# Two additions of the down-weight sums: from VectorE to GpSimd

## The chip, the cores and the metric

The kernel runs on one core of a Trainium2 chip. The metric is the device time of one execution in microseconds (us). The kernel before took 927.64 us, the median of three runs (927.62 to 928.56).

A core has four computing engines, each with its own queue of instructions in program order: TensorE (PE; PEld is its loading of weights), VectorE (DVE), ScalarE (ACT) and GpSimd (POOL). Instructions on different engines wait for each other through semaphores. DMA transfers are issued from the queues of SyncE (SP), ScalarE and GpSimd. TensorE writes to the banks of PSUM; the other engines read these banks or work on SBUF.

## The reference

Two decoder layers on an input of 512 x 1024. Layer 0 mixes by multi-scale causal pooling, layer 1 by differential attention. After each mixer comes a dense FFN, and after each of these four parts a LayerNorm of the scaled residual:

```python
def _swiglu(x, w_gate, w_up, w_down):
    return (jax.nn.silu(x @ w_gate) * (x @ w_up)) @ w_down

for i in range(DEPTH):
    h = _multiscale_pool(...) if i % 2 == 0 else _diff_attention(...)
    x = _layernorm(ALPHA * x + h, ln_mix_g[i], ln_mix_b[i])
    x = _layernorm(ALPHA * x + _swiglu(x, w_gate[i], w_up[i], w_down[i]), ln_ffn_g[i], ln_ffn_b[i])
```

The width of the FFN is 2816, all in float32. The change concerns the FFN, in both layers.

## The kernel before

**Products.** A float32 product is made of three matmuls of a reduced 32-bit type. Each operand is split into a high part (a cast, ScalarE) and a low part (the difference to the operand, VectorE): high x high, high x low, low x high, added up in a PSUM bank. So every 128x1024 piece of a weight costs a cast on ScalarE (L716 for gate and up) and a subtraction on VectorE (L719), ahead of its matmuls.

**Gate and up.** The hidden rows, 22 blocks of 128, are taken in units: plain ones, and nine double ones in which the 2x2 blocks of a product are made by seven products in place of eight (Strassen's way; `strassen`, L995). The seven are P1, Q5, P6, Q3, P7, P2 and Q4; the first two of the nine units have P1 and P2 made ahead and run five. The products of a unit are collected in three PSUM banks: A takes P1, P6, P7 and Q4 one after the other, C takes Q5 and Q3, B takes P2. Between them, other engines copy or combine what a bank holds so far: ScalarE copies A after P1 (L1015), C after Q5 (L1017) and A after P6 (L1019); VectorE reads C after Q3 (L1024) and A after P7 (L1026). TensorE may go on writing to a bank only when that reading is done. The matmuls of one of these products (`half_product`, L919) are 24 of 128x256. Sums of weight pieces for the products are made on VectorE (L713). All this is ordered by hand: what the other engines do is written between the products, with the preparation of weights some products ahead (`ahead`, `do_step`).

**The sums for the down product.** The product with w_down that follows is made by seven products as well. It needs sums of the four quarters of w_down, by rows of two blocks: W00+W01, W01+W11, W00+W01+W11 and W00+W01+W10+W11. They are made while gate and up run, and kept in DRAM (`tsum`) until they are read back. This goes in eleven steps for each FFN, k = 0 to 10:

- `load_terms(k)` (L812), from GpSimd's queue: two DMAs (L823) bring the quarters of step k into a tile of 128 x 2 x 2 x 512, then a third (L824) adds two quarters onto the first half while it loads. The tile is a part of the hidden buffer that is not yet in use for even k below 10 (`hid` in the trace), else a tile of its own (`b`).
- `sum_terms(k)` (L827): two additions of 128x512 (L829, L830), which make the last two sums out of the second half of the tile and what the third DMA left; the second reads what the first wrote.
- At the next `catch_up`, one product later: two DMAs to `tsum` from ScalarE's queue (L834). The first stores the first half of the tile, which the additions only read, and the second the half that they wrote. Then `load_terms(k + 2)` is issued.

The steps stand at the units and products in SUMMED (L53): behind the units f1, f2, f3, p3 and p4, and within p5 to p10 behind one of their products. Two tiles are under way at a time: loading of step k+1 is issued before the additions of step k stand in program order, loading of step k+2 after them.

GpSimd has little else to do in the FFN: its queue holds the loads and, at the end of each stage, a power of 128x1 for LayerNorm (L235). It takes a part in splitting elsewhere (L160 with `low=nc.gpsimd`).

Of the kernel before, what the change touches and what calls it, by code (L numbers as in the profile page):

```python
# [16 lines left out]
ALU = mybir.AluOpType  # L17
# [61 lines left out]
def trunk(ctx, tc, x, wall, pscale, lam_p, subln, table, lng, lnb, band, first, onehot, out):  # L79
    nc = tc.nc  # L80
# [489 lines left out]
    def ffn(layer, late):  # L570
# [6 lines left out]
        tt = nc.vector.tensor_tensor  # L577
        with tc.tile_pool(name=f"ffn{layer}", bufs=1) as fp:
# [230 lines left out]
            def term_slice(k):  # L809
                return slice(k % 2 * 512, (k % 2 + 1) * 512)  # L810

            def load_terms(k):  # L812
                if k < HALF - 1:
                    c = down + 4 * (k // 2)
                    src = wall[c : c + 4][:, :, term_slice(k)].rearrange("(j r) p t -> p j r t", j=2)
                else:
                    src = wall[down + 20 : down + 22].rearrange("j p (r t) -> p j r t", r=2)
                if k % 2 == 0 and k < HALF - 1:
                    t = rows_of[:, :, 9:11, :]
                else:  # L820
                    t = fp.tile([P, 2, 2, 512], F32, tag="b", name=f"b{layer}_{k}")
                for j in range(2):
                    nc.gpsimd.dma_start(out=t[:, j], in_=src[:, j])  # L823
                nc.gpsimd.dma_start(out=t[:, 0], in_=src[:, :, 1], accum_op=ALU.add)  # L824
                terms[k] = t

            def sum_terms(k):  # L827
                t = terms.pop(k)
                tt(t[:, 1, 1], t[:, 0, 0], t[:, 1, 1], op=ALU.add)  # L829
                tt(t[:, 1, 0], t[:, 1, 1], t[:, 1, 0], op=ALU.add)  # L830
                yield
                dst = tsum[:, k // 2, :, term_slice(k)].rearrange("(j r) p t -> p j r t", j=2)
                for j in range(2):
                    nc.scalar.dma_start(out=dst[:, j], in_=t[:, j])  # L834
                if k + 2 < HALF - 1:
                    load_terms(k + 2)
                if k == HALF - 2:
                    load_terms(HALF - 1)
# [4 lines left out]
            def weight_sums():  # L843
                g = sum_terms(summed_rows[0])
                summed_rows[0] += 1
                next(g)
                behind.append(g)
# [841 lines left out]
```

## Time and profile before

| | before |
|---|---|
| median of the runs | 927.64 us |
| range of the runs | 927.62 to 928.56 us |
| the profiled execution, its own time | 928.3 us |
| its span, first to last instruction | 926.5 us |
| mean granted TensorE clock | 0.998 |

The profile is of one execution. "Busy" is the time in which an engine had an instruction running. A row of a group gives line, engine, operation, tiles written and read, the shape and the count, then the busy time in us and the mean of one in ns, then the idle time of the engine just before it and what ended it. A row of the timeline gives start, duration, engine, line, operation, tiles and shapes, and in brackets the idle time before and who ended it. A row of the waits gives who waited for whom, and us in total, times, and the longest. A q behind an engine's name is its queue, which issues DMAs and waits. In tile names, numbers of buffers are left out, and g_28h and g_28l are the high and low part of weight piece 28 of an FFN.

### The profile page before, as it was taken

What the parts mean: (1) busy time and instruction counts of PE and PEld (TensorE: products, weight loads), DVE (VectorE), ACT (ScalarE), POOL (GpSimd) and SP (SyncE); (2) the same over time, 40 slices, a digit from 0 to 9 for tenths busy, and PEclk for the clock granted to TensorE, in tenths of its full rate; (3) what the DMA queues carried; (4) which work ended last, traced back from release to release, by engine and by line L of the source; (5) the groups of instructions that cost most, each with busy time, mean ns of one, the idle gap of its engine ahead of it and who ended that gap; (6) DMA issues with size and microseconds to landing.
All of it is one profiled execution on the core that took longest, in us unless ns stands there. A gap on an engine that the chain in (4) does not pass through costs nothing. (4 is left out here: it accounts for less than half of the span.)

```text
span 926.5 us, 15034 instructions
## 1 busy us (share of the span) xinstructions
PE 916.4 (99%) x5806; PEld 826.6 (89%) x5806; DVE 804.0 (87%) x1163; ACT 529.2 (57%) x841; POOL 110.3 (12%) x129
## 2 busy tenths in 40 slices
PE   9999999999999999999999999999999999999996
PEld 8999999999988888888888888989999999988885
DVE  7998798998899998868889786877798998899988
ACT  6773354444555657667878854843454444565551
POOL 4121121110100001101111100201111110100001
PEclk9999999999999999999999999999999999999999
DMA  8388988787766587975665622568878877756553
GB/s 235 119 285 235 296 254 248 256 249 241 219 215 192 188 251 226 227 206 151 163 144 120 155 90 69 162 225 257 264 195 289 279 251 236 220 195 206 193 203 103
DMA packets 72518, 192.50 MB, mean 208 GB/s; under 512 B 14548, under 2 KB 14804, under 8 KB 72446
## 3 DMA queue, kind: packets, MB, share of 16 engines
q1 hardware_dynamic: 44572, 121.36, 39.7%
q0 software_dynamic: 15712, 46.93, 22.5%
q10 hardware_dynamic: 12162, 23.25, 6.8%
q8 instruction: 45, 0.74, 0.3%
q14 instruction: 27, 0.22, 0.1%
HBM read 166.33 MB, written 25.19 MB: 207 GB/s over the span
## 5 line engine op out<-in xcount | busy, mean ns | idle before, releaser
L713 DVE TENSOR_TENSOR raw<-raw,raw 128x1024 f32<-128x1024 f32 x52 | 63.3, 1221 | 0.7
L160 DVE TENSOR_TENSOR xs<-hid,xs 128x512 fp32r<-128x512 f32 x84 | 53.7, 641 | 0.0
L159 ACT CAST xs<-hid 128x512 fp32r<-128x512 f32 x84 | 48.5, 580 | 0.4 <-DVE hid L1044 0.4
L1322 ACT ACTIVATE p<-p,mn 128x128 f32<-128x128 f32 (+3 forms) x64 | 35.2, 552 | 14.1 <-DVE mn L1317 14.1
L823 POOL DMA_DIRECT2D b<-in_wall x24 | 17.9, 793 | 144.1 <-DMA tsum<-b 33.9
L1317 DVE CUSTOM_DVE_ANT_0 p<-s,bias 128x128 f32<-128x128 f32 (+3 forms) x64 | 28.0, 485 | 1.1 <-PE s L1302 1.1
L823 POOL DMA_DIRECT2D hid<-in_wall x20 | 15.0, 751 | 111.7 <-DMA tsum<-hid 47.4
L1024 DVE TENSOR_TENSOR hid<-C,hid 128x512 f32<-128x512 f32 x18 | 12.4, 690 | 16.0 <-PE C L919 12.7
L235 POOL TENSOR_TENSOR rs<-rs,mhalf 128x1 f32<-128x1 f32 x16 | 12.5, 783 | 104.1 <-DVE rs L234 97.1
L1019 ACT COPY hid<-A 128x512 f32<-128x512 f32 x18 | 10.6, 586 | 24.9 <-PE A L919 24.9
L286 ACT ACTIVATE y<-pt,bT,gT 128x128 f32<-128x128 f32 x40 | 15.0, 456 | 15.9 <-PE pt L272 15.8
L1017 ACT COPY hid<-C 128x512 f32<-128x512 f32 x18 | 10.6, 588 | 22.2 <-PE C L919 17.2
L226 DVE BATCH_NORM_STATS2 st<-res 128x6 f32<-128x512 f32 x32 | 22.2, 695 | 1.1
L824 POOL DMA_DIRECT2D b<-in_wall x12 | 14.8, 1230 | 59.6 <-DMA b<-in_wall 59.6
L1026 DVE TENSOR_TENSOR hid<-hid,A 128x512 f32<-128x512 f32 x18 | 12.3, 682 | 10.6 <-PE A L919 10.6
L1031 ACT ACTIVATE sg<-A 128x512 f32<-128x512 f32 x18 | 10.7, 595 | 18.7 <-PE A L919 18.7
L1336 DVE SCALAR_TENSOR_TENSOR p<-p,sm,p 128x128 f32<-128x128 f32 (+3 forms) x32 | 17.6, 552 | 1.1
L713 DVE TENSOR_TENSOR more<-more,raw 128x1024 f32<-128x1024 f32 x15 | 18.3, 1220 | 0.2
L777 ACT CAST xs<-hid 128x1024 fp32r<-128x1024 f32 x8 | 8.4, 1052 | 14.3 <-DVE hid L786 8.7
L265 DVE TENSOR_TENSOR res<-res,gb 128x512 f32<-128x512 f32 (+1 forms) x20 | 16.0, 799 | 0.7
L160 POOL TENSOR_TENSOR sql<-sq,sqh 128x512 fp32r<-128x512 f32 x7 | 9.3, 1325 | 60.5 <-ACT sqh L159 60.5
L264 DVE TENSOR_TENSOR res<-res,gb 128x512 f32<-128x512 f32 (+1 forms) x20 | 15.8, 791 | 0.0
(1237 smaller groups left out, 3582.4 us busy)
## 6 DMA issues: line engine op xcount, KB each, us to landing
raw<-in_wall SPq DMA_DIRECT2D x120, 512.0 KB, 5.7
r<-tsum SPq DMA_DIRECT2D x40, 512.0 KB, 3.9
b<-in_wall POOLq DMA_DIRECT2D x36, 512.0 KB, 6.1
hid<-in_wall POOLq DMA_DIRECT2D x30, 512.0 KB, 5.8
r<-in_wall SPq DMA_DIRECT2D x30, 512.0 KB, 4.3
tsum<-b ACTq DMA_DIRECT2D x24, 512.0 KB, 4.4
tsum<-hid ACTq DMA_DIRECT2D x20, 512.0 KB, 5.8
more<-in_wall SPq DMA_DIRECT2D x10, 512.0 KB, 6.8
```

The lines of the kernel that those rows point to most:

```text
L159: nc.scalar.copy(dst_h, src)
L160: (low or nc.vector).tensor_tensor(dst_l, src, dst_h.bitcast(F32), op=ALU.subtract)
L226: nc.vector.bn_stats(stats[n, s][:, d, :], res[:, s, d * 512 : (d + 1) * 512])
L264: nc.vector.tensor_tensor(z, z, gb[:, 0, c], op=ALU.mult)
L265: nc.vector.tensor_tensor(z, z, gb[:, 1, c], op=ALU.add)
L286: nc.scalar.activation(y[:, k, :], pt[:, k * P : (k + 1) * P], AF.Identity, bias=bT[:, n, kk : kk + 1], scale=gT[:, n, kk : kk + 1],)
L713: tt(t, raws[pair[0]], raws[pair[1]], op=ALU.add)
L823: nc.gpsimd.dma_start(out=t[:, j], in_=src[:, j])
L824: nc.gpsimd.dma_start(out=t[:, 0], in_=src[:, :, 1], accum_op=ALU.add)
L1317: nc.vector.tensor_tensor_reduce(out=p, in0=accs[c], in1=biases[h][:, w - 1 :: -1] if w < S else biases[h][:, ::-1], op0=ALU.add, op1=ALU. ...
L1322: nc.scalar.activation(p, p, AF.Exp, bias=mn[:, q, c : c + 1], scale=-1.0, accum_out=sm[:, q, c : c + 1],)
L1336: nc.vector.scalar_tensor_tensor(p0[:, r], p0[:, r], sm[:, q, 0:1], p1[:, r], op0=ALU.mult, op1=ALU.add)
```

## The change

The two additions of `sum_terms` are issued to GpSimd instead of VectorE. Their operands, their place in program order and the DMAs around them stay as they are.

```diff
             def sum_terms(k):
                 t = terms.pop(k)
-                tt(t[:, 1, 1], t[:, 0, 0], t[:, 1, 1], op=ALU.add)
-                tt(t[:, 1, 0], t[:, 1, 1], t[:, 1, 0], op=ALU.add)
+                nc.gpsimd.tensor_tensor(
+                    t[:, 1, 1], t[:, 0, 0], t[:, 1, 1], op=ALU.add
+                )
+                nc.gpsimd.tensor_tensor(
+                    t[:, 1, 0], t[:, 1, 1], t[:, 1, 0], op=ALU.add
+                )
                 yield
                 dst = tsum[:, k // 2, :, term_slice(k)].rearrange("(j r) p t -> p j r t", j=2)
                 for j in range(2):
                     nc.scalar.dma_start(out=dst[:, j], in_=t[:, j])
                 if k + 2 < HALF - 1:
                     load_terms(k + 2)
```

`tt` is `nc.vector.tensor_tensor`.

## The prediction

> **What bounds the kernel now.** I read the page's busy times first, then who TensorE waited for, then the groups the diff touches.
>
> ```profile
> PE 916.4 (99%) x5806; PEld 826.6 (89%) x5806; DVE 804.0 (87%) x1163; ACT 529.2 (57%) x841; POOL 110.3 (12%) x129
> ```
> ```profile
> PE warm L392 <- POOL ident masks.py:199: 1.9, 1, 1.9
> PE pool L441 <- ACT fh L159: 0.2, 1, 0.2
> PE pt L272 <- DVE res L244: 0.2, 1, 0.2
> ```
> ```profile
> L829 DVE TENSOR_TENSOR b<-b 128x512 f32<-128x512 f32 x12 | 8.2, 686 | 0.0
> ...
> L829 DVE TENSOR_TENSOR hid<-hid 128x512 f32<-128x512 f32 x10 | 6.8, 685 | 0.0
> ```
> ```profile
> L160 POOL TENSOR_TENSOR sql<-sq,sqh 128x512 fp32r<-128x512 f32 x7 | 9.3, 1325 | 60.5 <-ACT sqh L159 60.5
> ```
>
> TensorE is busy 916.4 of 926.5 us. The second fence is everything it waited for: 1.9 + 0.2 + 0.2 = 2.3 us, none of it in the gate/up stage of either FFN, where the moved additions run. VectorE, at 87%, is second. So time that is only taken off VectorE is worth at most those 2.3 us, and in this stage nothing. What the change can do is spoil a hand-over that TensorE now just gets in time.
>
> **The change: what goes and what comes.** L829 ran 12 + 10 = 22 times, once for each step of the sums, and L830 with it: 44 additions of 128x512. VectorE loses them. The third fence below shows what a pair takes of its queue: L829 begins at 122.99, the operation behind the pair at 124.32, so 1.33 us, and 22 x 1.33 = 29 us in all. GpSimd gains them. The nearest row for their price there is its own 128x512 tensor_tensor, 1325 ns: 44 x 1.325 = 58 us on an engine busy for 110 of 926 us. No DMA is added or moved, but two queues change what they wait for.
>
> GpSimd's queue: the pair of step k now stands behind the accumulating load of step k+1 (L824) and ahead of the loads of step k+2. Those loads rewrite a buffer only when the second of ScalarE's stores (L834) has landed, which needed the additions before too. ScalarE's queue: that second store now waits for GpSimd instead of VectorE; behind it stand the casts of gate/up weights and the copies out of PSUM (L1015, L1017, L1019). VectorE waits for nothing new. In most steps GpSimd reaches the pair before VectorE did, since L824 of step k+1 is issued some microseconds ahead of step k's L829 and GpSimd has nothing else to do. Taken by itself the move costs nothing: what hides 2.65 us of GpSimd is the slack between L824 and the store.
>
> What is disputed is whether the two engines hinder each other.
>
> ```profile
> 14.25 1.22 DVE L160 TENSOR_TENSOR pw0l<-raw,pw0h 128x1024 fp32r<-128x1024 f32 x1
> ...
> 14.82 1.80 POOL L160 TENSOR_TENSOR xt<-res,xt 128x512 fp32r<-128x512 f32 x1 [2.13 <-ACT xt L159]
> ...
> 37.95 1.23 DVE L160 TENSOR_TENSOR w4l<-raw,w4h 128x1024 fp32r<-128x1024 f32 x1
> 38.17 1.41 POOL L235 TENSOR_TENSOR rs<-rs,mhalf 128x1 f32<-128x1 f32 x1 [9.57 <-DVE rs L234]
> ...
> 913.51 1.41 DVE L251 SCALAR_TENSOR_TENSOR res<-res,mv,gb 128x512 f32<-128x512 f32 x2
> ...
> 913.74 0.92 POOL L235 TENSOR_TENSOR rs<-rs,mhalf 128x1 f32<-128x1 f32 x1 [3.49 <-DVE rs L234]
> ...
> 914.84 1.41 DVE L255 SCALAR_TENSOR_TENSOR res<-res,rs,gb 128x512 f32<-128x512 f32 x2
> ```
>
> A GpSimd operation that meets a VectorE operation with two SBUF inputs waits for that one to end: the 128x1 power started at 38.17 ends at 39.58, 0.40 us after VectorE's 39.18; the 128x512 subtraction ends at 16.62, which is 1.15 us after VectorE's 15.47. So GpSimd is held until the operation in progress ends, and then needs 1.15 us. At 913.74 it got in between two such operations that followed each other closely, so it isn't starved. Whether VectorE is held in turn, no row shows: none has VectorE starting a two-input operation inside a full GpSimd one. (The pair at 913.51 took 1.41 us, as the pair at 914.84 did without GpSimd, but a 128x1 read is too short to tell.) The bounds for one addition are 0 (no hold) and 1.15 us. Here almost all of VectorE's work has two SBUF inputs (L713, L719, L1044, L1045). I take 1.15, because a wait that lasts to the very end of the other's instruction looks like exclusive ownership, and that would be mutual.
>
> The Trainium skill, "SBUF — State Buffer", section "Who interferes with whom", says that a VectorE instruction with two SBUF inputs contends with a GpSimd instruction that reads SBUF, and that the one issued second blocks fully. The trace agrees for GpSimd's half (the 0.40 us above); no run here shows VectorE's half. By that rule the sum is the one with 1.15, without it the one with 0.
>
> With alternating turns a pair takes from VectorE's queue 2 x 1.15 = 2.30 us and gives back 1.33: a net 0.97 us late behind the place of the removed pair, and up to 2.30 ahead of it. Weight preparation can bear that. Four hand-overs of a PSUM bank can't.
>
> Step 7: the additions fall between L1024 and L1026, where nothing was removed.
>
> ```profile
> 189.67 1.23 POOL L824 DMA_DIRECT2D hid<-in_wall  x1 [2.83 <-DMA hid<-in_wall]
> ```
> ```profile
> 190.95 0.69 DVE L1024 TENSOR_TENSOR hid<-C,hid 128x512 f32<-128x512 f32 x1 [1.79 <-PE C L919]
> 191.56 2.48 DVE L713 TENSOR_TENSOR raw<-raw,raw 128x1024 f32<-128x1024 f32 x2
> 193.95 1.22 DVE L719 TENSOR_TENSOR g_51l<-raw,g_51h 128x1024 fp32r<-128x1024 f32 x1
> 195.09 0.68 DVE L1026 TENSOR_TENSOR hid<-hid,A 128x512 f32<-128x512 f32 x1
> ```
> ```profile
> 196.44 0.40 PE L919 MATMUL A<-xt,g_49h 128*128 128x256 f32 x2
> ```
>
> The first starts at 190.90 and ends at 192.2; L713 is held from 191.56, 0.65 us. The second takes its turn behind that L713, another 1.15. L1026 ends 1.80 later than 195.77; TensorE wants bank A at 196.44, 0.67 later. Stall 1.80 - 0.67 = 1.1 us.
>
> Step 3: ScalarE's copy out of bank C hangs on a cast, the cast on VectorE's L713.
>
> ```profile
> 120.68 1.23 POOL L824 DMA_DIRECT2D hid<-in_wall  x1 [2.37 <-DMA hid<-in_wall]
> ```
> ```profile
> 122.99 0.69 DVE L829 TENSOR_TENSOR b<-b 128x512 f32<-128x512 f32 x1
> ...
> 124.32 1.22 DVE L713 TENSOR_TENSOR more<-more 128x1024 f32<-128x1024 f32 x1
> ```
> ```profile
> 125.63 1.05 ACT L716 CAST g_28h<-more 128x1024 fp32r<-128x1024 f32 x1 [2.46 <-DVE more L713]
> ...
> 126.58 0.59 ACT L1017 COPY hid<-C 128x512 f32<-128x512 f32 x1
> ```
> ```profile
> 127.22 0.39 PE L919 MATMUL C<-xs,g_25h 128*128 128x256 f32 x1
> ```
>
> GpSimd is free at 121.91, in the run of two-input operations ahead of 122.99. L713, and with it the cast and the copy, comes 0.97 later; the copy now ends at 127.17, 0.05 ahead of TensorE. Stall 0.9.
>
> Step 5 is the same chain with the copy out of bank A, step 6 has ScalarE's store in it.
>
> ```profile
> 154.40 1.23 POOL L824 DMA_DIRECT2D hid<-in_wall  x1 [2.71 <-DMA hid<-in_wall]
> ```
> ```profile
> 155.31 2.36 DVE L713 TENSOR_TENSOR raw<-raw,raw 128x1024 f32<-128x1024 f32 x2
> ```
> ```profile
> 162.66 1.05 ACT L716 CAST g_42h<-raw 128x1024 fp32r<-128x1024 f32 x1 [1.92 <-DVE raw L713]
> ...
> 163.67 0.57 ACT L1015 COPY B<-A 128x512 f32<-128x512 f32 x1
> ```
> ```profile
> 164.76 0.40 PE L919 MATMUL A<-xs,g_38h 128*128 128x256 f32 x2
> ```
> ```profile
> 175.80 1.25 POOL L824 DMA_DIRECT2D b<-in_wall  x1 [4.88 <-DMA b<-in_wall]
> ```
> ```profile
> 179.80 0.69 DVE L830 TENSOR_TENSOR hid<-hid 128x512 f32<-128x512 f32 x1
> ```
> ```profile
> 180.99 0.60 ACT L1042 ACTIVATE sg<-B 128x512 f32<-128x512 f32 x1 [3.09 <-DVE hid L830]
> ...
> 183.85 0.60 ACT L1015 COPY B<-A 128x512 f32<-128x512 f32 x1
> ```
> ```profile
> 184.92 0.40 PE L919 MATMUL A<-xs,g_45h 128*128 128x256 f32 x2
> ```
>
> Step 5: GpSimd is free at 155.63, inside the L713 pair; the cast comes 0.97 late, the copy ends 0.52 ahead of TensorE: stall 0.45. Step 6: free at 177.05, the additions end after 0.8 + 1.15 + 1.22 + 1.15, at 181.4, where L830, for which ScalarE waited, ended at 180.5; 0.9 late less the 0.47 between the copy's end and TensorE: 0.45.
>
> Step 1: VectorE is idle there, but GpSimd is late.
>
> ```profile
> 84.44 1.27 POOL L824 DMA_DIRECT2D hid<-in_wall  x1
> ```
> ```profile
> 84.81 0.59 ACT L1017 COPY hid<-C 128x512 f32<-128x512 f32 x1 [2.29 <-PE C L919]
> ```
> ```profile
> 87.49 0.40 PE L919 MATMUL C<-xs,g_13h 128*128 128x256 f32 x2
> ```
>
> If L824 stays where it is, the pair ends at 85.71 + 2.65 = 88.4, ScalarE copies until about 89.3 and TensorE loses 1.8 us. But L824 will come some 2 us earlier: it stood behind a load that waited for a store that waited for VectorE. Bounds 0 and 1.8; I take 0.3, nearer to the early end, in the first FFN alone.
>
> The other steps (0, 2, 4, 8, 9, 10) I count as nothing: their additions meet weight preparation that runs microseconds ahead of TensorE. Sum for one FFN: 1.1 + 0.9 + 0.45 + 0.45 = 2.9; twice, 5.8; with step 1, 6.1 us. The profiled execution took 928.3 us (span 926.5), 0.7 above the median of 927.64: 934.4 for it, 933.7 for the median.
>
> **The rivals.**
> *VectorE is never held.* The place is the same four hand-overs, the price of an addition is 0, and it decides from a hold of about 0.6 us an addition down, where 2 x 0.6 is less than the 1.33 given back. Then chains 3, 5 and 6 come earlier, which buys nothing where TensorE didn't wait; only step 1 is left: 927.64 + 0.3 = 927.9, no change. For it: the unlengthened pair at 913.51. Against it: GpSimd's own waits.
>
> *GpSimd is starved.* If back-to-back two-input operations kept it out, step 5 would have to wait from 155.63 to the next pause of VectorE:
>
> ```profile
> 170.79 0.69 DVE L1024 TENSOR_TENSOR hid<-C,hid 128x512 f32<-128x512 f32 x1 [2.04 <-PE C L919]
> ```
>
> VectorE pauses at 168.75; the additions would end at 171.4, the store's wait holds ScalarE behind the cast of 162.66, and the copy due by 164.76 comes some 7 us late. For ten steps of each FFN that would be 140 us, for half of them 70: some 1000. Against it: GpSimd got in at 913.74.
>
> *VectorE's relief becomes time.* That needs TensorE to wait for VectorE, and it does for 0.2 us in all: at best 927.4, no change; a real gain would need something the trace doesn't show.
>
> **How the numbers follow.** The hold with alternating turns 0.60, VectorE never held 0.30, starvation 0.07, a gain from the relief 0.03. About 0.2% (1.9 us) is what a measurement of this kernel can tell from no change. Of the 0.60, 0.05 ends inside that (only one addition of a pair hits, 0.5 us on step 7 and little else); of the 0.30, 0.01 ends above. Slower 0.55 + 0.01 + 0.07 = 0.63; within 0.05 + 0.29 = 0.34; faster 0.03. The predicted time is 933.7. Its own range is 929 (one hold in a pair) to 943 (eight steps of each FFN lose about 1 us each: 16 us on top of 927.6). The range given reaches down over the case without hold: 927.2 to 943. Outside are starvation and the ends, some 0.15.
>
> **What would show it.** GpSimd's L829 and L830 with means well above 1325 ns (1.6 to 2.4 us with the waiting); VectorE's L713 and L719 with means above 1220, by up to 1.15 us on some 40 instructions, so that its busy time falls by less than 29 us or rises; TensorE waiting for L1026, L1017 and L1015, some 6 us in all. If L713 and L719 keep 1220 ns and GpSimd's additions alone are long, the hold is one-sided and the first rival is right. If ScalarE's waits for L830 grow from 3 to 8 us, it is starvation. The prediction is wrong if the time stays under 929.

## The result and the profile after

The changed kernel takes 943.15 us (median of four executions, 940.89 to 944.03), the kernel before beside it on the same chip 927.99 us (927.62 to 928.56). The ratio is 1.0158, with a 95% interval of 1.0145 to 1.017: slower by 15 us, where 6 were forecast. The profiled execution took 940.89 us with a span of 939.1, 12.6 more than the span before.

In the changed kernel the two additions are L829 and L832, and every line behind them is four higher: the store L834 is L838, the matmul L919 is L923, the copies L1015, L1017 and L1019 are L1019, L1021 and L1023, the VectorE operations L1024, L1026, L1044 are L1028, L1030, L1048.

The busy times of the page after:

```profile
PE 918.1 (98%) x5806; PEld 826.2 (88%) x5806; DVE 820.4 (87%) x1119; ACT 529.3 (56%) x841; POOL 185.8 (20%) x173
```

VectorE has 44 instructions fewer, and is busy for 820.4 us. The kernel in which the additions are left out on both engines (e1 below) shows what would be left:

```profile
PE 916.2 (99%) x5806; PEld 826.5 (89%) x5806; DVE 776.4 (84%) x1119; ACT 530.3 (57%) x841; POOL 110.5 (12%) x129
```

The difference to its 776.4 us, 44.0 us, is time in which VectorE's instructions were held: 1.00 us for each of the 44 additions that run on GpSimd. The groups of the page show on both engines where it is (the last two numbers ahead of the second bar are busy us and the mean in ns):

```profile
L713 DVE TENSOR_TENSOR raw<-raw,raw 128x1024 f32<-128x1024 f32 x52 | 72.5, 1397 | 0.9
...
L829 POOL TENSOR_TENSOR b<-b 128x512 f32<-128x512 f32 x12 | 22.4, 1866 | 19.2 <-DMA b<-in_wall 19.2
...
L832 POOL TENSOR_TENSOR b<-b 128x512 f32<-128x512 f32 x12 | 24.5, 2044 | 0.9
```

GpSimd's additions take 1.87 and 2.04 us on the tile `b` (1.78 and 1.85 on `hid`). A pair takes about 4.0 us, not 2.65. TensorE's waits, from the view of who waited for whom (total us, times, longest):

```profile
PE C L923 <- ACT hid L1021: 5.2, 3, 2.2
PE A L923 <- ACT B L1019: 3.1, 2, 2.9
...
PE A L923 <- ACT hid L1023: 1.5, 2, 1.0
PE A L923 <- DVE hid L1030: 1.0, 3, 0.4
```

These 10.8 us are new; the three waits of before (2.3 us) are still there. By the starts of the matmuls (how much later than its usual pitch each matmul of L923 began) it is 13.9 us, in these steps of the sums:

| step | 1 | 2 | 3 | 4 | 5 | 6 | 7 | 8, 9 | sum |
|---|---|---|---|---|---|---|---|---|---|
| first FFN | 2.44 | 0.68 | 1.54 | 0 | 0.31 | 0 | 0.66 | 0.49 | 6.1 |
| second FFN | 0 | 1.31 | 2.03 | 0.53 | 3.13 | 0 | 0.63 | 0.19 | 7.8 |
| forecast, both | 0.3 | 0 | 1.8 | 0 | 0.9 | 0.9 | 2.2 | 0 | 6.1 |

The span grew by 12.6 us only. This execution was 0.9 us ahead of the one before already in front of its first FFN, where the matmuls of L441 followed each other faster, and some 0.3 us of the 13.9 was lost at the same places before.

Step 3 of the first FFN shows how one of them comes about. The timeline of GpSimd, then VectorE, ScalarE and TensorE (start us, duration us, engine, line):

```profile
120.46 1.23 POOL L824 DMA_DIRECT2D hid<-in_wall  x1 [0.68 <-DMA hid<-in_wall]
121.24 1.77 POOL L829 TENSOR_TENSOR b<-b 128x512 f32<-128x512 f32 x1
123.09 2.17 POOL L832 TENSOR_TENSOR b<-b 128x512 f32<-128x512 f32 x1
...
121.12 2.98 DVE L719 TENSOR_TENSOR g_25l<-raw,g_25h 128x1024 fp32r<-128x1024 f32 x1
124.03 2.31 DVE L719 TENSOR_TENSOR g_24l<-more,g_24h 128x1024 fp32r<-128x1024 f32 x1
...
127.93 1.22 DVE L713 TENSOR_TENSOR more<-more 128x1024 f32<-128x1024 f32 x1
...
129.23 1.05 ACT L716 CAST g_28h<-more 128x1024 fp32r<-128x1024 f32 x1 [3.88 <-DVE more L713]
...
130.19 0.58 ACT L1021 COPY hid<-C 128x512 f32<-128x512 f32 x1
...
130.82 0.50 PE L923 MATMUL C<-xs,g_25h 128*128 128x256 f32 x2 [1.28 <-ACT hid L1021]
```

Both instructions of VectorE take 1.22 us elsewhere; here the first takes 2.98 and the second 2.31, together 2.85 us of hold. Each ends about 1.1 us after one of GpSimd's additions. The removed pair would have stood directly ahead of the L713 at 127.93, so 1.33 us are given back there: 2.85 - 1.33 = 1.52 us late. TensorE had 0.05 us to spare in the profile before, and comes 1.41 later than there (1.54 by the table, 1.28 as the row counts its idle time).

The first of the two is remarkable: it began at 121.12, before the addition's own start at 121.24, and was held for 1.76 us. In other steps it is more. The hold by the first addition reaches 2.1 to 2.3 us where an instruction of VectorE starts soon after L824's issue; from step 1:

```profile
83.08 1.23 POOL L824 DMA_DIRECT2D hid<-in_wall  x1 [1.98 <-DMA hid<-in_wall]
83.85 1.78 POOL L829 TENSOR_TENSOR b<-b 128x512 f32<-128x512 f32 x1
85.71 2.13 POOL L832 TENSOR_TENSOR b<-b 128x512 f32<-128x512 f32 x1
...
83.43 3.30 DVE L713 TENSOR_TENSOR more<-more,raw 128x1024 f32<-128x1024 f32 x1
...
87.88 0.37 ACTq L838 DMA_DIRECT2D tsum<-b  x1
88.28 0.58 ACT L1021 COPY hid<-C 128x512 f32<-128x512 f32 x1 [6.68 <-DMA tsum<-b]
...
88.92 0.50 PE L923 MATMUL C<-xs,g_13h 128*128 128x256 f32 x2 [2.18 <-ACT hid L1021]
```

The L713 starts 0.42 us ahead of the first addition, and yet ends 1.1 us behind its end. The pair is done at 87.84; ScalarE, idle for 6.68 us, issues its store then and copies bank C behind it, and TensorE loses 2.4 us.

How a hold becomes a stall can be read where several runs lose time at the same hand-over. At step 3 of the second FFN the pair held VectorE for 3.22 us in the changed kernel, 2.52 in e3 and 2.19 in e9 (both below), and TensorE lost 1.90, 1.19 and 0.86 us against the profile before: each time the hold less 1.33, which is what the removed pair gives back. At step 2 of that FFN it was 3.01, 2.81 and 2.18 us of hold and 1.31, 1.10 and 0.48 us of stall: the hold less 1.70. What counts at these two is the sum of a pair's holds, above an amount that the hand-over can bear, whatever the pieces (the longest was 2.13 us in the changed kernel and 1.10 in e9). Elsewhere that amount differs between the runs: at step 7 of that FFN it was 0.52 us in e3 and e9 and 1.16 in the changed kernel.

### The profile page after: what moved, and what is told of

It reads as the page before. It is cut to its first block, busy times and chain, and to the rows that moved or that the text cites. A ratio compares the mean times of both kernels' runs of the same rounds, so it can differ in the third digit from the quotient of the medians.

```text
span 939.1 us, 15021 instructions
## 1 busy us (share of the span) xinstructions
PE 918.1 (98%) x5806; PEld 826.2 (88%) x5806; DVE 820.4 (87%) x1119; ACT 529.3 (56%) x841; POOL 185.8 (20%) x173
## 5 line engine op out<-in xcount | busy, mean ns | idle before, releaser
L713 DVE TENSOR_TENSOR raw<-raw,raw 128x1024 f32<-128x1024 f32 x52 | 72.5, 1397 | 0.9
L160 DVE TENSOR_TENSOR xs<-hid,xs 128x512 fp32r<-128x512 f32 x84 | 54.6, 652 | 0.0
L235 POOL TENSOR_TENSOR rs<-rs,mhalf 128x1 f32<-128x1 f32 x16 | 12.7, 795 | 104.1 <-DVE rs L234 98.9
L1023 ACT COPY hid<-A 128x512 f32<-128x512 f32 x18 | 10.5, 586 | 28.1 <-PE A L923 28.1
L829 POOL TENSOR_TENSOR b<-b 128x512 f32<-128x512 f32 x12 | 22.4, 1866 | 19.2 <-DMA b<-in_wall 19.2
L824 POOL DMA_DIRECT2D b<-in_wall x12 | 14.8, 1230 | 55.6 <-DMA b<-in_wall 55.6
L1028 DVE TENSOR_TENSOR hid<-C,hid 128x512 f32<-128x512 f32 x18 | 12.4, 688 | 14.3 <-PE C L923 13.3
L832 POOL TENSOR_TENSOR b<-b 128x512 f32<-128x512 f32 x12 | 24.5, 2044 | 0.9
L286 ACT ACTIVATE y<-pt,bT,gT 128x128 f32<-128x128 f32 x40 | 15.0, 455 | 15.9 <-PE pt L272 15.8
L1030 DVE TENSOR_TENSOR hid<-hid,A 128x512 f32<-128x512 f32 x18 | 12.3, 681 | 11.9 <-PE A L923 9.7
L713 DVE TENSOR_TENSOR more<-more,raw 128x1024 f32<-128x1024 f32 x15 | 22.0, 1468 | 0.2
L160 POOL TENSOR_TENSOR sql<-sq,sqh 128x512 fp32r<-128x512 f32 x7 | 9.3, 1325 | 60.5 <-ACT sqh L159 60.5
L1021 ACT COPY hid<-C 128x512 f32<-128x512 f32 x18 | 10.6, 588 | 18.8 <-PE C L923 12.1
L1035 ACT ACTIVATE sg<-A 128x512 f32<-128x512 f32 x18 | 10.7, 596 | 16.0 <-PE A L923 15.8
L342 POOL DMA_DIRECT2D tall<-in_wall x2 | 2.4, 1207 | 84.7 <-DVE xs L160 84.7
```

Source lines behind the costliest of these rows:

```text
L160: (low or nc.vector).tensor_tensor(dst_l, src, dst_h.bitcast(F32), op=ALU.subtract)
L235: nc.gpsimd.tensor_tensor(rs, rs, mhalf, op=ALU.pow)
L286: nc.scalar.activation(y[:, k, :], pt[:, k * P : (k + 1) * P], AF.Identity, bias=bT[:, n, kk : kk + 1], scale=gT[:, n, kk : kk + 1],)
L713: tt(t, raws[pair[0]], raws[pair[1]], op=ALU.add)
L829: nc.gpsimd.tensor_tensor(t[:, 1, 1], t[:, 0, 0], t[:, 1, 1], op=ALU.add)
L832: nc.gpsimd.tensor_tensor(t[:, 1, 0], t[:, 1, 1], t[:, 1, 0], op=ALU.add)
```

## The experiments

Three readings were open: that VectorE's hold is the cause, that ScalarE's longer wait at its store is, and, once the trace was seen, that the place of the pair is: on GpSimd it runs well ahead of where VectorE would have come to it. The times of before beside the runs were 927.94 to 928.18 us.

**e1: no additions at all.** Both lines of the pair are left out on both engines, so the sums lack two of their terms.

> This kernel is the one before without the two additions: they are left out altogether, on either engine, and the stores write what the loads left. It asks what VectorE's relief alone is worth. Relief worth nothing (TensorE never waited for VectorE): the time of before, 927.5 to 928.5. Relief worth something: 926 or less. The holding theory and the waiting theory expect the same here.

Measured: 927.85 us, ratio 0.9996 (0.9987 to 1.0005). VectorE's relief by itself is worth nothing.

**e2: memsets in place of the pair.** GpSimd is kept as long, but by operations that only write; the sums are left out.

```diff
+                for _ in range(4):
+                    nc.gpsimd.memset(t[:, 1], 0.0)
```

> In place of the two additions GpSimd fills the same half of the tile four times with zeros (the sums are left out): about 4 x 0.9 = 3.6 us of GpSimd for each step, near the 4.1 us of the pair in the changed kernel, at the same place in its queue and with the same store waiting for it, but GpSimd reads no SBUF. If VectorE is held by GpSimd's reading, the operations of VectorE keep their 1220 ns and the time falls to 928 to 931 (the wait of step 1 may stay). If the loss came from ScalarE's store waiting for a late GpSimd, the time stays at 938 to 943.

Measured: 930.14 us, ratio 1.0033 (1.0016 to 1.0049). The groups of this kernel:

```profile
L830 POOL MEMSET b<- 128x1024 f32 x48 | 49.9, 1039 | 2.1
...
L713 DVE TENSOR_TENSOR raw<-raw,raw 128x1024 f32<-128x1024 f32 x52 | 63.3, 1221 | 0.9
```

Four memsets take 4.2 us, as long as the pair, and L713 keeps its 1221 ns. So it is the reading of SBUF by GpSimd that holds VectorE, and the 15 us need that hold: all that a slow GpSimd does at ScalarE's store costs about 2 us here. The Trainium skill ("SBUF — State Buffer", "Who interferes with whom") says that a VectorE instruction with two SBUF inputs contends with a GpSimd instruction that reads SBUF and not with one that only writes it; both halves are seen here, 1397 against 1221 ns.

**e3: the later store from GpSimd's queue.** ScalarE then waits for no addition.

```diff
-                    nc.scalar.dma_start(out=dst[:, j], in_=t[:, j])
+                    (nc.gpsimd if j else nc.scalar).dma_start(out=dst[:, j], in_=t[:, j])
```

> The changed kernel, but the second store of each step is issued from GpSimd's own queue, behind the additions, so ScalarE waits for GpSimd nowhere. Holding theory: VectorE is held as before (some 2 us for each pair), only the loss of step 1 (2.4 us) and little else goes: 938 to 941. Waiting theory: 928 to 931.

Measured: 939.66 us (936.87 to 940.87), ratio 1.012 (1.0097 to 1.0144). Taking ScalarE's wait away gives back 3.5 of the 15 us; VectorE is busy for 823.2 us, held as before. The hold, with the pair where it is, is worth some 12 us. Step 1 of the first FFN, which lost 2.4 us in the changed kernel, loses nothing here.

**e4: only the second addition on GpSimd**, the first back on VectorE.

> Only the second of the two additions is on GpSimd, the first is back on VectorE. Holding theory: one hold for each step, and since that addition waits for VectorE's it can't be taken up while GpSimd still issues the load ahead of it, so about 1.1 us of hold in place of 2.0, against 0.6 us given back: 929 to 933. Waiting theory: the store still waits for GpSimd, which now starts after VectorE and so ends later than in the changed kernel in most steps: 938 or more.

Measured: 935.31 us, ratio 1.0084 (1.0069 to 1.0099). Now GpSimd has to wait for VectorE's L829, and no hold is above 1.1 us. But TensorE waits for ScalarE again, and the timeline of ScalarE and GpSimd in step 6 shows why:

```profile
178.34 5.51 ACTq L836 DMA_DIRECT2D tsum<-hid  x2
...
181.26 2.20 POOL L830 TENSOR_TENSOR hid<-hid 128x512 f32<-128x512 f32 x1 [4.72 <-DVE hid L829]
```

The store's issue is held until the addition ends at 183.46, 2.20 us of GpSimd where VectorE's L830 took 0.69. All that stands behind it on ScalarE is late, up to the copy out of bank A, for which TensorE waits 1.0 us. It lies between the two theories: the hold costs little here, the wait at the store does.

**e5: the pair behind VectorE's place.** As e3, and VectorE copies one column of the first operand onto itself ahead of the pair, so that GpSimd can't start before VectorE's queue has come to where the pair stood.

```diff
+                nc.vector.tensor_copy(t[:, 0, 0, :1], t[:, 0, 0, :1])
                 nc.gpsimd.tensor_tensor(
```

> The changed kernel with its second store issued from GpSimd's queue (as e3_own_store), and one instruction more in each step: VectorE copies the first column (128x1) of the pair's first operand onto itself just ahead of the pair, so that GpSimd's first addition must wait for VectorE's queue to come to that place and no longer stands right behind the issue of L824. All results are computed. Theory A (an addition that stands right behind a DMA issue of GpSimd holds VectorE from the start of that issue, 1.7 to 2.3 us, and an addition that doesn't holds it for 1.1): VectorE is held 1.1 us by each of the two additions, some 2.2 a pair and never above 1.2 on one instruction, L713's and L719's long ones stop at 2.35 us, and the time falls under e3's 939.7, to 931-937. Theory B (the first addition holds VectorE up to 2.3 us wherever it stands): ones of 2.9 to 3.4 us stay and the time is 938-942.

Measured: 931.98 us (929.52 to 932.08), ratio 1.0035 (1.0022 to 1.0048): 7.7 us less than e3, for an instruction of 0.15 us more in each step. Timeline of GpSimd, then VectorE:

```profile
160.82 2.26 POOL L830 TENSOR_TENSOR b<-b 128x512 f32<-128x512 f32 x1 [2.39 <-DVE b L829]
163.16 2.15 POOL L833 TENSOR_TENSOR b<-b 128x512 f32<-128x512 f32 x1
...
160.58 0.15 DVE L829 COPY b<-b 128x1 f32<-128x1 f32 x1
160.70 1.22 DVE L713 TENSOR_TENSOR raw<-raw,raw 128x1024 f32<-128x1024 f32 x1
161.84 2.32 DVE L719 TENSOR_TENSOR g_40l<-raw,g_40h 128x1024 fp32r<-128x1024 f32 x1
164.09 1.78 DVE L1049 TENSOR_TENSOR hid<-sg,hid 128x512 f32<-128x512 f32 x1
```

Here the engines take turns as the prediction had it: addition, VectorE's instruction, addition. VectorE's instructions are held by 1.1 us each (2.32 for 1.22 us, 1.78 for 0.69), the additions by 0.9 to 1.0 (one that meets nothing takes 1.29 us). In five of the 22 steps the pair still stands right behind L824, which came after VectorE's copy there, and one instruction is held for 1.2 to 1.9 us. VectorE is held 40 us in all, nearly as long as in e3 (47). So either the length of the single hold counts, or that it now falls behind the old place of the pair; e9 and e10 were to change one of these each.

**e6: e4 with the later store from GpSimd's queue.**

> Only the second addition is on GpSimd (as e4_second_only), and the second store is issued from GpSimd's queue in place of ScalarE's. All results are computed. In e4 TensorE waited 3.9 us for ScalarE's copy out of bank A and 2.0 for that out of bank C. Theory A (those are ScalarE waiting at its store for GpSimd; a hold of 1.1 us by one addition, behind which VectorE has given back 0.6, costs TensorE nothing): VectorE's held instructions stay at about 2.32 us, TensorE's waits for L1017 and L1019 go, time 927.5-930. Theory B (the hold of VectorE makes them, through the casts): the waits stay, 933-936.

Measured: 931.01 us, ratio 1.0027 (1.0015 to 1.0039), and TensorE's waits for the copies are gone; 1.4 us for VectorE's reading of bank A (L1026 before, L1028 here) stay. It is 4.3 us better than e4: those were ScalarE's wait. The time is 1 us above the range of the first theory, and two holds are longer than it had them, 2.15 and 1.82 us: in steps 1 and 8 of the first FFN the addition came right behind the issue of L824.

**e7: the store alone**, with the additions on VectorE.

> The kernel before, additions on VectorE, with the second store of each step issued from GpSimd's queue in place of ScalarE's: the control for the three kernels that move it. All theories: VectorE is not held (L713, L719 at 1220 ns), and TensorE loses nothing, 927.3-928.7. If it is above that, the moved store has a cost of its own which has to be taken off the other three; if it is below, ScalarE's wait cost time before as well.

Measured: 927.28 us, ratio 0.9996 (0.9987 to 1.0006). The moved store costs nothing and gains nothing.

**e8, e11, e13: only the first addition on GpSimd.** e8 is the mirror image of e4; e11 moves the later store as e3 does; e13 also puts the memsets of e9 in front.

> Only the first addition of each pair is on GpSimd, the second is back on VectorE (the mirror image of e4_second_only), the stores are ScalarE's. All results are computed. VectorE now has to wait for GpSimd's addition before its own. Theory A (right behind L824 the hold is up to 2.3 us): in most steps one L713 or L719 takes 2.9 to 3.4 us, VectorE is held some 30 us in all by 22 additions, where e4's 22 additions held it 1.1 each, 24 in all; less ScalarE delay than e4 has: 929-936. Theory B (1.1 each wherever it stands): no instruction over 2.4 us, 928-931.

> As e8_first_only (only the first addition on GpSimd, right behind L824, the second on VectorE; 938.4 us), with the second store issued from GpSimd's queue. All results are computed. In e8 the additions hold VectorE 25.7 us ahead of the place where VectorE's first addition stood, in single holds of up to 2.3 us; in e9 the pairs hold it 22.7 us ahead of that place, in single holds of 1.1 at most (932.7 us). Theory A (what counts is how much hold falls ahead of the old place, whatever its pieces): without ScalarE's wait this one comes to e9's time, 931.5-934. Theory B (a single hold of 1.7 to 2.3 us costs more than two of 1.1): 935-938.

> As e11_first_own_store (only the first addition on GpSimd, second store from its queue; 939.8 us), with the four memsets of e9 between the issue of L824 and that addition. All results are computed. Theory A (the single long hold right behind L824 costs e11 its 11.8 us): the holds fall to 1.1 at most and the time to 928-932, under e9's 932.7, since half as many additions hold VectorE. Theory B (the holds' length is not what matters: VectorE is given back only half as much where the second addition stays with it, and e11 pays for that): 936-940.

Measured: e8 938.37 us (ratio 1.011, 1.0095 to 1.0125), e11 939.76 (1.0123, 1.0108 to 1.0138), e13 940.58 (1.0149, 1.0125 to 1.0172). The holds went as the first theories had it, up to 2.26 us in e8 (over 1.25 in 11 of its 22 steps) and none above 1.2 in e13. The times didn't follow: shorter holds made nothing faster. The groups of VectorE name what no expectation had in it (the last column is the idle time before the line and its releaser), first e8, then e13:

```profile
L832 DVE TENSOR_TENSOR b<-b 128x512 f32<-128x512 f32 x12 | 8.2, 686 | 6.1 <-POOL b L829 5.9
L832 DVE TENSOR_TENSOR hid<-hid 128x512 f32<-128x512 f32 x10 | 6.9, 686 | 6.8 <-POOL hid L829 6.8
```
```profile
L835 DVE TENSOR_TENSOR b<-b 128x512 f32<-128x512 f32 x12 | 8.2, 685 | 13.7 <-POOL b L832 13.6
L835 DVE TENSOR_TENSOR hid<-hid 128x512 f32<-128x512 f32 x10 | 6.8, 684 | 9.0 <-POOL hid L832 9.0
```

VectorE's own addition waits for GpSimd's: 12.7 us in e8, 17.1 in e11, 22.6 in e13, where the memsets delay GpSimd further. With fewer additions on GpSimd than in the whole pair, e11 is no faster than e3 (939.8 and 939.7 us) and e13 slower than e9 below (940.6 and 932.7); only e8, with the store on ScalarE, is faster than the changed kernel (938.4 and 943.2). So the split pair gains less than its smaller hold would give, and its own wait is what is new in it. Of the question for which e11 and e13 were made, the length of a hold against its place, they say nothing.

**e9: memsets between L824 and the pair.** As e3, with four memsets of 128x128 on GpSimd in front of the pair.

> As e3_own_store (both additions on GpSimd, second store from its queue, 939.7 us), with four memsets of a 128x128 scratch tile on GpSimd between the issue of L824 and the pair. All results are computed. The pair stays as early as in e3, well ahead of VectorE's old place for it, but no longer stands right behind a DMA issue; memsets alone didn't hold VectorE (e2). Theory A (the issue right in front is what makes the long hold): L713 and L719 stop at about 2.35 us, VectorE is held some 1.1 by each addition, 931-936. Theory B (what e5 gained came from the later place of the pair, behind VectorE's own work, and not from what stood in front of it): instructions of 2.9 to 3.4 us stay, 937-942.

Measured: 932.74 us (931.92 to 932.98), ratio 1.0048 (1.0033 to 1.0063). GpSimd and VectorE in step 5:

```profile
153.56 1.23 POOL L824 DMA_DIRECT2D hid<-in_wall  x1 [2.17 <-DMA hid<-in_wall]
154.31 1.49 POOL L831 MEMSET pad<- 128x128 f32 x4
155.77 1.87 POOL L832 TENSOR_TENSOR b<-b 128x512 f32<-128x512 f32 x1
...
156.40 2.33 DVE L719 TENSOR_TENSOR g_39l<-raw,g_39h 128x1024 fp32r<-128x1024 f32 x1
```

The pair is still 5.3 us ahead of its old place (median over the steps; 7.6 in e3), but no instruction of VectorE is held for more than 1.1 us, and all holds together fall from 47 to 32 us. Operations that do nothing make the kernel 6.9 us faster than e3.

**e10: a DMA issue in front of the late pair.** As e5, with the copied column sent to a scratch tile from GpSimd's queue just ahead of the pair.

> As e5_add_behind_vector (the pair waits for VectorE's 128x1 copy, 932.0 us), with one more DMA issue on GpSimd right in front of the pair: that column copied to a scratch tile, which has to wait for VectorE's copy as well. All results are computed. The pair keeps the late place of e5, but stands right behind a DMA issue again. Theory A: the first addition takes 1.77 us again and VectorE instructions of 2.9 to 3.4 us come back, about one for each step; 936-941. Theory B: VectorE's longest stay at about 2.35 us and the time at 931-934 (with some us more if the issue, about 0.8 us, makes the pair too late).

Measured: 931.15 us (929.94 to 932.68), ratio 1.0039 (1.0025 to 1.0053). Steps 5 and 10 on GpSimd, then VectorE's instruction in each:

```profile
162.02 1.23 POOL L824 DMA_DIRECT2D hid<-in_wall  x1 [2.76 <-DMA hid<-in_wall]
162.77 1.07 POOL L831 DMA_DIRECT2D tick<-b  x1
163.37 1.79 POOL L832 TENSOR_TENSOR b<-b 128x512 f32<-128x512 f32 x1
...
255.62 0.57 POOL L831 DMA_DIRECT2D tick<-b  x1 [10.78 <-DVE b L829]
256.21 1.32 POOL L832 TENSOR_TENSOR b<-b 128x512 f32<-128x512 f32 x1
...
163.20 2.52 DVE L1052 TENSOR_TENSOR hid<-sg,hid 128x512 f32<-128x512 f32 x1
...
255.90 2.72 DVE L160 TENSOR_TENSOR d_2l<-r,d_2h 128x1024 fp32r<-128x1024 f32 x1
```

L1052 (L1045 before) takes 0.69 us elsewhere, L160 in this form 1.22. Both began while a DMA issue ran on GpSimd and ahead of the addition behind it, and both ended behind the addition's end, by 0.56 us the 128x512 and by 1.09 the 128x1024. The second stands behind the small issue alone, so it isn't L824 as such: what VectorE started during the issue was held until the addition was done, and longer behind the longer issue. Eight steps have such holds of over 1.25 us, up to 2.26; in the others VectorE's instruction had begun ahead of the issue, the addition waits for it, and the next one is held for 1.1. The theory is right on the mechanism, and wrong on the time: at 43 us of hold it is that of e5, so late long holds cost no more here than late short ones.

**e12: the column copy alone.** The changed kernel with e5's copy, both stores left with ScalarE.

> The changed kernel with VectorE's 128x1 copy of a column of the pair's first operand onto itself ahead of the pair, and nothing else: both stores stay ScalarE's. All results are computed. Theory A (the pair's early place makes most of the 15.5 us, ScalarE's wait for the later store some 3-6 of what is left): the hold is all behind the old place as in e5, and the time is e5's 932.0 and ScalarE's wait, which is longer here than in the changed kernel since the pair starts later: 935-940. Theory B (the early place doesn't matter where ScalarE waits anyway): 942-946.

Measured: 968.29 us (965.98 to 969.5), ratio 1.0425 (1.0408 to 1.0443): worse than either theory, and 36 us worse than e5, from which it differs by the queue of one store. The busy times of the page, TensorE's waits, and ScalarE's timeline in step 6:

```profile
PE 930.0 (96%) x5806; PEld 836.9 (87%) x5806; DVE 802.2 (83%) x1141; ACT 528.1 (55%) x841; POOL 194.5 (20%) x173
```
```profile
PE C L924 <- ACT hid L1022: 14.3, 8, 5.0
PE A L924 <- ACT B L1020: 12.8, 6, 2.7
```
```profile
190.24 4.95 ACTq L839 DMA_DIRECT2D tsum<-hid  x2
195.29 0.60 ACT L1047 ACTIVATE sg<-B 128x512 f32<-128x512 f32 x1 [6.40 <-POOL hid L833]
...
198.14 0.60 ACT L1020 COPY B<-A 128x512 f32<-128x512 f32 x1
```

GpSimd begins where VectorE used to begin, and takes 4 us or more where VectorE took 1.3; ScalarE stands at its store for that long, and so do the copies that TensorE needs (L1020 and L1022 here are L1015 and L1017 before). The waits for these copies come to 27.1 us. Another 13.6 us, which the expectation had nothing of, is TensorE's own busy time, 930.0 us for 916.4 before, at a granted clock that fell to one half six times (last section).

All runs with an addition on GpSimd, side by side. "Ahead" and "behind" is the time for which VectorE's instructions were held (each one's duration less the usual one of its form), ahead of or behind the old place of the pair in VectorE's order:

| | hold ahead, us | behind, us | later store | time, us |
|---|---|---|---|---|
| changed kernel | 39.5 | 4.8 | ScalarE | 943.15 |
| e3 | 40.9 | 6.3 | GpSimd | 939.66 |
| e9, memsets between | 22.7 | 9.1 | GpSimd | 932.74 |
| e5, pair late | 0 | 40.4 | GpSimd | 931.98 |
| e10, pair late, issue in front | 0 | 43.3 | GpSimd | 931.15 |
| e6, second only | 0 | 20.2 | GpSimd | 931.01 |
| e4, second only | 0 | 14.6 | ScalarE | 935.31 |
| e12, pair late | 0 | 24.2 | ScalarE | 968.29 |
| e8, e11, e13, first only | 25.7, 22.0, 15.8 | 0 | ScalarE, GpSimd, GpSimd | 938.4, 939.8, 940.6 |

With the later store on GpSimd and the pair whole, the time doesn't follow the hold in all: 40 us behind the old place cost 3 to 4, 41 ahead of it cost 12. It isn't proportional to the hold ahead either: 22.7 us of that, with 9.1 behind, cost e9 only 0.7 us more than e5. That fits the steps above, where a hand-over bears an amount of hold and what is above it becomes a stall: in e9 a pair holds VectorE for 2.2 us at most, in e3 for up to 3.35. With the store on ScalarE a late pair costs more than an early one. The early pair pays in hold, the late one at the store.

## Why the prediction was wrong

*That VectorE is held* was right, and an addition that takes its turn holds it for 1.1 us, against the 1.15 taken. That the mean over all 44 is near as well, 1.00 us, is partly luck: the first additions of the pairs hold it for nothing to 2.27 us, the second for nothing to 1.10. e2 shows that the hold needs GpSimd's reads. The rival in which VectorE is never held falls with L713's 1397 ns, and starvation falls too: no addition took longer than 2.36 us in any run, its waiting included.

*That the relief is worth nothing* was right (e1).

*The net of a pair, "2 x 1.15 = 2.30 us and gives back 1.33: a net 0.97 us late"*, is the step that failed. The hold by one addition isn't always 1.15: the first one, behind L824, held VectorE for up to 2.27 us, so that a pair took up to 3.36. The prediction let the addition begin at the end of L824's issue; its row begins 0.78 us into the issue of 1.23 us, and VectorE is shut out from still earlier. And the 1.33 us come back at the old place of the pair, which the pair on GpSimd precedes by 7.6 us in the median. The prediction said that the pair is up to 2.30 us late ahead of that place, and used it in step 7 alone. What VectorE and, through the casts, ScalarE owe TensorE in between is late by the hold with nothing given back: at step 7 of the second FFN e3 and e9 lost 1.55 and 1.57 us for holds of 2.07 and 2.08, and the changed kernel 0.63 for 1.79, so that in all three less than the 1.33 was made up. Step 3 is the clean case: net 1.52 in place of 0.97, and a stall of 1.4 to 1.5 in place of 0.9. In step 5 of the second FFN the forecast 0.45 became 3.13: hold of 3.08 us, and behind it a store issue which kept ScalarE 1.25 us more. Where the engines take turns and the hold falls behind the old place, as the net has it, in e5, the cost was 4.0 us, against the 5.8 forecast.

*"The other steps (0, 2, 4, 8, 9, 10) I count as nothing"*: steps 2, 4, 8 and 9 lost 3.2 us over both FFNs. Weight preparation runs ahead, but a hold of 2 to 3 us is more than ScalarE's copies out of bank A (steps 2 and 4) and VectorE's reading of that bank (8 and 9) have to spare. At step 2 of the second FFN the 2.30 us of the prediction would have been too much as well: above 1.70 it becomes a stall.

*Step 1, "I take 0.3"*: 2.44, above the upper bound of 1.8. L824 came 1.36 us earlier by the rows (83.08 for 84.44), but TensorE was 0.91 us earlier there too, so 0.45 us is left in place of 2. The pair took 4.0 us in place of 2.65, since it too is held. By TensorE's time it was done 0.35 us later than the upper bound had it (87.84 + 0.91 = 88.75, for 88.4).

*Step 7* was forecast at 1.1 and lost 0.66 and 0.63; *step 6*, forecast at 0.45, lost nothing. TensorE was 3.9 us later by then, and so the forecast end of the pair, 181.4, is 185.3 there; it ended at 184.59.

*"Taken by itself the move costs nothing: what hides 2.65 us of GpSimd is the slack between L824 and the store"* was wrong by 3.5 us (e3 against the changed kernel): with 4 us the slack doesn't reach.

The terms add up: 6.1 forecast; steps 1, 3 and 5 came to 2.1, 1.8 and 2.5 more, steps counted as nothing to 3.2, steps 6 and 7 to 1.8 less: 13.9 us of stalls in the profiled execution. The median lies 2.3 us above that execution; where the others lost these was not traced.

What stays open: whether, over a whole kernel, an early hold costs more in one long piece than in two short ones of the same sum. At the two hand-overs of the second FFN compared above it doesn't. But e9 made the holds shorter and fewer at once (and moved part of them behind the old place), and the runs that were to separate the two met VectorE's own wait instead. By what an issue that is still running lets the addition behind it keep VectorE out is open as well.

## What to carry to other kernels

Work that is moved to an idle engine runs at another time than it did, and a hold that it puts on the old engine doesn't fall where the time is given back: price the hold at what is due between the two places, and compare it with what each hand-over there can bear, not as a net over both. Moved work that is slower and feeds a store holds up whatever else is queued behind that store's issue: move the issue with it, or count the new wait. And a pair of dependent operations split over two engines brings a wait of its own.

## What the runs showed of the hardware

GpSimd's addition can hold VectorE from before its recorded start, while the DMA issue ahead of it is still running: an L713 that began 0.42 us ahead of the addition took 3.30 us for 1.22. Behind a smaller issue (0.57 us) it was 2.72 us for 1.22 (e10). Four memsets of 0.32 us each in between, or a place away from an issue, bring the hold back to 1.1 us. In the changed kernel twelve instructions of VectorE began during an issue of L824 that had an addition right behind it: seven were held for 1.73 to 2.27 us, four that began within 0.03 us of the issue's start were not, nor was one that reads a bank of PSUM (L1030, begun at 740.87, 0.35 us into the issue: 0.68 us, as ever). The Trainium skill ("GPSIMD Engine Reference", "2.1 Instruction dispatch") says that consecutive instructions on this engine are no barrier between its cores, each of which starts the next one when its own share is done. That would fit an addition that begins in part under the issue, but no run here shows it.

Only instructions that read both their inputs from SBUF were held. In all runs together VectorE's readings of banks A and C (L1028 and L1030 in the changed kernel), which have one input in PSUM, ran beside an addition for 0.3 us or more 52 times, and none was held.

TensorE's clock can drop after a short wait. The table of windows has the granted clock as the third number from the end, of e12, of e11, and of the changed kernel, each right behind a wait of TensorE (2.73, 1.78 and 2.87 us):

```profile
198.70:203.00 4.30, 4.21 (x22) 4.21 (x23) 3.71 (x4) 1.50 (x3) 0.18 (x1) 0.60 0.66 261
```
```profile
112.60:117.00 4.40, 4.36 (x24) 4.36 (x25) 2.40 (x4) 0.48 (x1) 0.76 (x1) 0.61 1.00 365
```
```profile
730.60:735.00 4.40, 4.40 (x36) 4.40 (x37) 3.18 (x3) 1.99 (x3) 0.00 (x0) 1.00 1.01 337
```

The granted clock is its mean over the window. In e12 it is 0.50 from 199.4 to 202.8 and in e11 from 113.6 to 117.0, and 22 and 24 matmuls go through these windows where the third row has 36; in the changed kernel the longest wait was followed by none of this. So a wait can cost TensorE about 1.7 us beyond itself (3.41 us at half the clock), and its length alone doesn't decide. In e12 there are six such stretches, 27.3 us together, and TensorE is busy for 930.0 us, 12 more than in the changed kernel, for the same matmuls.

The traces point to what decides. Within a trace the clock changes lie whole multiples of 3.41 us apart. On that grid, e12's six drops came after windows of 3.41 us in which TensorE was busy for shares of 0.01, 0.20, 0.25, 0.07, 0.25 and 0.44, and e11's after one of 0.48. No window of 0.49 or more was followed by a drop in any of the traces, and of those between 0.45 and 0.48 only e11's was. The wait of 2.87 us in the changed kernel is cut in two by the grid, at 728.8, and leaves windows of 0.68 and 0.47. The Trainium skill ("TensorE: Matmul & The Clock Gate", "Part 1: The HAM clock gate") has the clock halved after an idle window of about 3.4 us that runs freely. The halving, the length and the free running fit these traces; the waits that brought it here, 1.78 and 2.73 us, are shorter than such a window, so it needn't be idle throughout.
